# Strassen attention on one core: the order of the P·V products, the tiles that hold P, and the start

## The chip, the core and the metric

The kernel runs on one core of a Trainium2 chip. The core has a matrix engine (TensorE; PE for its matmuls, PEld for its weight loads), VectorE (DVE), ScalarE (ACT), GpSimd (POOL, which here issues the loads) and SyncE (SP, which here issues the stores and the DMA transpositions). Each engine runs its instructions in program order; between engines there are semaphores. The metric is the device time of one execution in microseconds (us).

## The reference

```
q, k, v: (8, 2048, 512) float32
scores = q @ k.transpose(0, 2, 1) / sqrt(512)
out    = softmax(scores, axis=-1) @ v          # (8, 2048, 512) float32
```

No maximum is taken off before the exp in the kernel; the sums of the exps come out of the second product, through a column of ones beside v.

## The kernel before

**Tiles.** A step g is one batch and 512 queries (32 steps, four to a batch). Its transposed probabilities P (2048 keys by 512 queries, fp16) are made block by block from QK products and lie in one tile `pt`, indexed by key block pair j, key half s and query. P times V gives four output blocks of 128 queries by 512, handled as two pairs, a and b.

**Winograd's form of Strassen.** Both matrix products replace eight half-size products by seven. So there are seven QK products for a group of four key blocks (class `Group`, 4 matmuls each, line 246, four groups a step) and seven PV products for a pair (class `Pair`, 8 matmuls each, line 328). DVE makes the sums and differences of blocks that serve as operands: of P in `p_sums` (s1, s2, a21 in place, s4, lines 289 to 293), of q, k and v in `q_sums`, `k_sums`, `v_sums` (the background sums). Several products of one pair add into the same PSUM bank, and between them the bank is read:

- bank x: products 1, 4, 6, 7; ACT scales it into the output after 3, 6 and 4, DVE adds it after 7
- bank z: products 5 and 3; ACT scales it after 5 (a DVE reciprocal of the row sums comes first), DVE takes another reciprocal after 3 and adds z after 6
- bank y: product 2; DVE adds it after 2

The scaling is line 336 (ACT), the add line 339 (DVE), the reciprocals lines 351 and 357. A pair's x comes from a ring of two banks; y and z have one bank each for both pairs.

**The main loop.** Step g's PV products run beside step g+1's QK products. A period has 28 slots. Each slot has one QK product in the order of `QORDER` (seven to a group, products 7 and 4 of a group one group later, as `prev`), and each odd slot has a PV product of `ORDER`, behind the QK product. After each QK product its reader is issued: copies by ACT (lines 259, 263, 266), adds by DVE (269, 272), exps by ACT (197; `exp_right` for two query halves at a time). The last group of a step ends in slots 0 to 5 of the next period.

**Loads.** `PLAN` gives slots to loads, transpositions (`dma_transpose`, line 112) and background sums, whose operations are issued one at a time in slots 0, 2, 3 and 6 of each seven. GpSimd and SyncE don't follow the slots: they run ahead as far as waits allow. q and k pass through a ring of staging tiles; v goes straight into `vh` (two buffers). `new_v` writes the column of ones into a new `vh` by a memset (line 168), and that memset waits until every reader of the buffer's old tile is done; the loads behind it on GpSimd's queue wait too. A step's q is loaded three steps ahead.

**The start.** q's first two blocks and k's first four are transposed by PE (line 125). Steps 0 and 1 are computed without Strassen (`plain_tile`, 4 matmuls of 512 columns and one exp a key block). Then step 0's remaining PV products run alone, and the main loop begins.

Of the kernel before, what the change touches and what calls it, by code (L numbers as in the profile page):

```python
# [12 lines left out]
def kernel(  # L13
# [21 lines left out]
    nc = tc.nc  # L35
    P = 128
    B, T, D = q.shape
# [22 lines left out]
    COPY = mybir.ActivationFunctionType.Copy  # L60

    const = ctx.enter_context(tc.tile_pool(name="const", bufs=1))
    stage = ctx.enter_context(tc.tile_pool(name="stage", bufs=3))
    kpool = ctx.enter_context(tc.tile_pool(name="kpool", bufs=5))
    qpool = ctx.enter_context(tc.tile_pool(name="qpool", bufs=3))
    vpool = ctx.enter_context(tc.tile_pool(name="vpool", bufs=2))
# [28 lines left out]
        "v": v.rearrange("b (n p) d -> b p n d", p=P),  # L95
    }

    def load(what, b, c):
        t = stage.tile([P, CH, D], F16, tag="stage")
        nc.gpsimd.dma_start(out=t[:], in_=srcs[what][b, :, c * CH:(c + 1) * CH, :])  # L100
        staged[what, b, c] = t

    def operands(what):
# [83 lines left out]
        ]  # L187

    def new_p(g):
        pt = ppool.tile([P, NJ, 2, QTW], F16, tag="pt")  # L190
        s1 = ppool.tile([P, NJ, QH], F16, tag="s1")
        s2 = ppool.tile([P, NJ, QH], F16, tag="s2")
        s4 = ppool.tile([P, NJ, QH], F16, tag="s4")
        pts[g] = (pt, s1, s2, s4)

    def exp(out_, in_):
        nc.scalar.activation(out=out_, in_=in_, func=EXP, scale=inv_sqrt_d)  # L197
# [1 line left out]
    def plain_tile(g, kb):  # L199

        b, qt = divmod(g, NQT)
        if kb == 0:
            new_p(g)
        st = bank("qz" if kb % 3 == 2 else "qx")
        c, n = divmod(kb, CH)
        for dc in range(ND):
            nc.tensor.matmul(
                st[:], kT[b, c][0][:, n, dc, :], qT[b, qt][0][:, :, dc, :],
                start=(dc == 0), stop=(dc == ND - 1),
            )  # L210
        exp(pts[g][0][:, kb // 2, kb % 2, :], st[:])

    class Group:

# [7 lines left out]
        def product(self, n):  # L222
            a11, a12, a21, a22 = k_blocks(self.a)
            b11, b12, b21, b22 = q_blocks(self.b)
            _, s1, s2, s4 = self.a
            _, t1, t2, t4 = self.b
            if n == 1:
                if self.n == 0:
                    new_p(self.g)
                self.pt = pts[self.g][0]  # L230
                self.x = bank("qx")
            elif n == 5:
                self.z = bank("qz")
            lhs, rhs, dst = {
                1: (a11, b11, "x"),
                2: (a12, b21, "y"),
                3: (s4, b22, "z"),
                4: (a22, t4, "x"),
                5: (s1, t1, "z"),
                6: (s2, t2, "x"),  # L240
                7: (a21, b12, "x"),
            }[n]
            dst = getattr(self, dst)
            for j in range(G):
                for c in range(2):
                    nc.tensor.matmul(  # L246
                        dst[:, j * QH:(j + 1) * QH], lhs[:, j, c, :], rhs[:, :, c, :],
                        start=(n in (1, 5) and j == 0 and c == 0), stop=(c == 1),
                        skip_group_check=True,
                    )  # L250
            getattr(self, f"after{n}", lambda: None)()
# [20 lines left out]
            nc.vector.tensor_add(self.cz[:, :, 0, :], self.two(self.z), self.cz[:, :, 0, :])  # L272

        def after4(self):
            exp(self.pt[:, self.js, 1, 0:QH], self.two(self.x))

        def after2(self):
            exp(self.pt[:, self.js, 0, 0:QH], self.two(self.y))

        def exp_right(self):  # L280
            exp(self.pt[:, self.js, :, QH:QTW], self.cz[:])

    def p_sums(g, n, part=None):
        pt, s1, s2, s4 = pts[g]
        js = slice(n * G, (n + 1) * G)
        a11, a21 = pt[:, js, 0, 0:QH], pt[:, js, 0, QH:QTW]
        a12, a22 = pt[:, js, 1, 0:QH], pt[:, js, 1, QH:QTW]
        if part in (None, 0):
            nc.vector.tensor_add(s1[:, js], a21, a22)  # L289
            nc.vector.tensor_sub(s2[:, js], s1[:, js], a11)  # L290
            nc.vector.tensor_sub(a21, a11, a21)  # L291
        if part in (None, 1):
            nc.vector.tensor_sub(s4[:, js], a12, s2[:, js])  # L293

    class Pair:

        def __init__(self, g, i):
            self.g, self.i = g, i  # L300

        def product(self, n):
            g, i = self.g, self.i
            pt, s1, s2, s4 = pts[g]
            vh, t1, t2, t4 = vs[g // NQT]
            c1 = slice(i * P, (i + 1) * P)
            c2 = slice(QH + i * P, QH + (i + 1) * P)
            if n == 1:
                self.x = bank("px")
            elif n == 2:  # L310
# [1 line left out]
            elif n == 5:  # L312
                self.z = bank("pz")
            lhs, rhs, dst = {
                1: (lambda j: pt[:, j, 0, c1], lambda j: vh[:, j, 0, 0:H], "x"),
                2: (lambda j: pt[:, j, 1, c1], lambda j: vh[:, j, 1, 0:H], "y"),
                3: (lambda j: s4[:, j, c1], lambda j: vh[:, j, 1, H:D + 1], "z"),
                4: (lambda j: pt[:, j, 1, c2], lambda j: t4[:, j, :], "x"),
                5: (lambda j: s1[:, j, c1], lambda j: t1[:, j, 0:H + 1], "z"),
                6: (lambda j: s2[:, j, c1], lambda j: t2[:, j, :], "x"),  # L320
                7: (lambda j: pt[:, j, 0, c2], lambda j: vh[:, j, 0, H:D], "x"),
            }[n]
            dst = getattr(self, dst)
            width = H + 1 if n in (3, 5) else H
# [18 lines left out]
        def store(self, o, half):  # L343
            b, qt = divmod(self.g, NQT)
            n = qt * NQS + half * (NQS // 2) + self.i
            nc.sync.dma_start(out=out[b, n * P:(n + 1) * P, :], in_=o[:])

        def after5(self):
            self.o2 = opool.tile([P, D], F32, tag="o")
            self.r2 = small.tile([P, 1], F32, tag="r2")  # L350
# [8 lines left out]

        def after2(self):  # L360
            self.final(self.o1[:, 0:H], self.y[:, 0:H], self.r1)

        def after6(self):
            self.scaled(self.o1[:, H:D], self.x[:, 0:H], self.r1)
            self.final(self.o1[:, H:D], self.z[:, 0:H], self.r1)
            self.store(self.o1, 0)

        def after7(self):
            self.final(self.o2[:, H:D], self.x[:, 0:H], self.r2)
# [2 lines left out]
            self.scaled(self.o2[:, 0:H], self.x[:, 0:H], self.r2)  # L372
            self.store(self.o2, 1)

    ORDER = "a1 b1 a5 a3 a2 a6 a7 b5 a4 b3 b2 b6 b7 b4".split()

    QORDER = ((0, 1), (1, 7), (0, 5), (0, 6), (1, 4), (0, 3), (0, 2))
    NS = len(QORDER) * NG
# [1 line left out]

    PLAN = {}
    for qt_, slot_, *what_ in (
        (0, 0, "newv"),
# [10 lines left out]
    for qt_ in range(NQT):  # L396
        PLAN.setdefault((qt_, 0), []).append(("load", "q", 3))
        PLAN.setdefault((qt_, 10), []).append(("trans", "q", 3))
        PLAN.setdefault((qt_, 15 if qt_ == 3 else 12), []).append(("sum", "q", 2))
    background = deque()  # L400

    def prefetch(g, slot):
        b, qt = divmod(g, NQT)
# [21 lines left out]


    NP = B * NQT
    load("q", 0, 0)
    load("k", 0, 0)
    load("k", 0, 1)  # L430
    dummy = bank("qy")
    pe_transpose("q", 0, 0)
    pe_transpose("k", 0, 0)
    load("k", 0, 2)
    load("k", 0, 3)
    new_v(0)
    nc.tensor.matmul(dummy[:], ident[:], kT[0, 0][0][:, 0], start=True, stop=True)
    load("q", 0, 1)
    for kb in range(NKB):
        plain_tile(0, kb)  # L440
# [1 line left out]
            pe_transpose("k", 0, kb // CH + 1)  # L442
        if kb % (2 * G) == 0 and kb:
            p_sums(0, kb // (2 * G) - 1)
        if kb == 3:
            load_v(0, 0)
        if kb == 7:
            load_v(0, 1)
        if kb == 11:
            load_v(0, 2)  # L450
            load_v(0, 3)
            load("q", 0, 2)
            load("q", 0, 3)
    pe_transpose("q", 0, 1)
    p_sums(0, NG - 1)

    pairs = (Pair(0, 0), Pair(0, 1))

    def pv(g, n):
        pairs[ORDER[n][0] == "b"].product(int(ORDER[n][1]))  # L460

    for kb in range(NKB):
        plain_tile(1, kb)
        if kb == 3:
            dma_transpose("q", 0, 2)
        if kb == 4:
            dma_transpose("q", 0, 3)
        if 6 <= kb < 14 and kb % 2 == 0:
            for f in v_sums(0, (kb - 6) // 2):
                f()  # L470
        if kb % (2 * G) == 0 and kb:
            p_sums(1, kb // (2 * G) - 1)
        if kb >= 14:
            pv(0, kb - 14)
    p_sums(1, NG - 1)
    for n in range(2, len(ORDER)):
        pv(0, n)
        if n < 6:
            for f in k_sums(0, n - 2):
                f()  # L480
        if n == 6:
            for f in q_sums(0, 2):
                f()
        if n == 7:
            for f in q_sums(0, 3):
                f()

    prev = None
    for g in range(1, NP):
        pairs = (Pair(g, 0), Pair(g, 1))  # L490
        for slot in range(NS):
            if g + 1 < NP:
                n, at = divmod(slot, len(QORDER))
                if at == 0:
                    cur = Group(g + 1, n)
                old, what = QORDER[at]
                if old == 0:
                    cur.product(what)
                elif prev is not None:
                    prev.product(what)  # L500
            elif slot in (1, 4):
                prev.product(QORDER[slot][1])
            if g + 1 < NP or slot < 7:
                at = slot % len(QORDER)
                if prev is not None:
                    if at == 2:
                        prev.exp_right()
                    if at == 4:
                        p_sums(prev.g, prev.n, 0)
                    if at == 5:  # L510
                        p_sums(prev.g, prev.n, 1)
                if at == len(QORDER) - 1 and g + 1 < NP:
                    prev = cur
            if slot % 2 == 1:
                pv(g, slot // 2)
            prefetch(g, slot)


# [28 lines left out]
```

## Time and profile before

| | us |
|---|---|
| median of 3 runs (lowest, highest) | 881.41 (880.58, 881.64) |
| the profiled execution | 881.62 |
| its span, first to last instruction | 879.5 |
| PE busy | 811.9 |
| DVE busy | 585.2 |
| ACT busy | 568.5 |

The rows are of that one execution. A row of the timeline gives start, duration, engine, source line, operation, tiles as out<-in, shapes, how many instructions were merged, and in brackets how long the engine stood idle before and which instruction's end released it. Matmuls overlap: the duration of a row ends later than the next row begins.

### The profile page before, as it was taken

The page shows a single profiled execution, that of the slowest core. Times are in us where ns is not written, and L with a number is a line of the kernel's source. Part 1 is how long each engine was busy: PE and PEld are TensorE (multiplying, and loading weights), DVE is VectorE, ACT ScalarE, POOL GpSimd, SP SyncE. Part 2 cuts the span into 40 slices and gives each one's busy share as a digit, 9 for nine tenths or more (in the row PEclk, how much of TensorE's full clock was granted, in tenths as well). Part 3 has the DMA queues.
Part 4 walks back from the last instruction along what each step waited for, and adds up shares of the span by engine and source line. Part 5 has one row for each costly group of instructions (what it writes and reads, how often), then busy time and mean ns, then how long its engine had stood idle before and what let it go on. Part 6 is the DMA issues. An engine that isn't in the chain of part 4 may idle for free.

```text
span 879.5 us, 18122 instructions
## 1 busy us (share of the span) xinstructions
PE 811.9 (92%) x7169; PEld 697.8 (79%) x7169; DVE 585.2 (67%) x1460; ACT 568.5 (65%) x1009; POOL 72.9 (8%) x116
## 2 busy tenths in 40 slices
PE   6979999999999999999999999999999999999997
PEld 4458878888887888888888888888888888888885
DVE  3675776776766777666776667767766767756653
ACT  2626666667666667666676676676676676666772
POOL 3200102001020000200001000200002000000000
PEclk9999999999999999999999999999999999999999
DMA  9994885948779593996939759296794958921101
GB/s 145 203 176 103 164 135 107 200 95 149 124 140 184 112 155 95 159 162 126 159 80 178 160 111 182 67 202 124 141 148 89 205 91 156 168 61 49 49 31 67
DMA packets 189989, 115.50 MB, mean 131 GB/s; under 512 B 124368, under 2 KB 173520, under 8 KB 189904
## 3 DMA queue, kind: packets, MB, share of 16 engines
q0 software_dynamic: 50688, 50.34, 37.9%
q1 hardware_dynamic: 139216, 64.01, 34.7%
q8 instruction: 56, 0.92, 0.4%
q14 instruction: 29, 0.24, 0.1%
HBM read 100.70 MB, written 33.55 MB: 153 GB/s over the span
## 4 chain that ended last, share of the span: by engine, by line
PE 61%; DVE 15%; ACT 14%; DMA 6%; issue 4%; POOL 0%; POOLq 0%; DVEq 0%; ACTq 0%
PE t L328 33%; PE t L246 28%; ACT pt L197 7%; ACT o L336 5%; DVE o L339 4%; DMA raw<-t 2%; DVE cz L272 2%; ACT cz L263 2%; DVE cz L269 2%; DMA t<-in_q_dram 2%; DVE s L289 2%; DMA t<-in_k_dram 2%; DVE pt L291 1%; DVE s L293 1%; DVE s L290 1%
## 5 line engine op out<-in xcount | busy, mean ns | idle before, releaser
L328 PEld LDWEIGHTS <-pt 128*128 128x128 f16 x2048 | 199.8, 98 | 71.8 <-issue 48.6
L336 ACT ACTIVATE o<-t,r 128x256 f32<-128x256 f32 x256 | 121.3, 474 | 171.1 <-DVE r L351 82.9
L328 PE MATMUL t<-vh,pt 128*128 128x256 f16 x1536 | 198.9, 273 | 14.0 <-ACT o L336 14.0
L197 ACT ACTIVATE pt<-t 128x512 f16<-128x512 f32 x272 | 163.6, 601 | 72.1 <-PE t L246 46.7
L246 PEld LDWEIGHTS <-raw 128*128 128x128 f16 x1920 | 187.7, 98 | 22.1
L246 PE MATMUL t<-raw 128*128 128x256 f16 x1440 | 196.7, 273 | 0.0
L328 PEld LDWEIGHTS <-s 128*128 128x128 f16 x1536 | 149.9, 98 | 42.7 <-issue 23.1
L246 PEld LDWEIGHTS <-ks 128*128 128x128 f16 x1440 | 140.8, 98 | 16.5
L339 DVE SCALAR_TENSOR_TENSOR o<-t,r,o 128x256 f32<-128x256 f32 x192 | 92.5, 482 | 91.9 <-ACT o L336 67.3
L246 PE MATMUL t<-qs,ks 128*128 128x256 f16 x960 | 134.3, 273 | 0.0
L328 PE MATMUL t<-t,s 128*128 128x257 f16 (+1 forms) x1024 | 133.1, 273 | 0.8 <-DVE o L339 0.8
L197 ACT ACTIVATE pt<-cz 128x1024 f16<-128x1024 f32 x120 | 127.4, 1061 | 2.3 <-DVE cz L269 1.1
L289 DVE TENSOR_TENSOR s<-pt 128x512 f16<-128x512 f16 x128 | 54.1, 423 | 95.7 <-ACT pt L197 95.7
L269 DVE TENSOR_TENSOR cz<-t,cz 128x512 f32<-128x512 f32 x120 | 82.5, 687 | 19.9 <-PE t L246 19.9
L263 ACT COPY cz<-t 128x512 f32<-128x512 f32 x120 | 70.1, 584 | 37.9 <-PE t L246 33.3
L328 PE MATMUL t<-t,pt 128*128 128x256 f16 x512 | 66.3, 272 | 22.8 <-DVE o L339 21.6
L272 DVE TENSOR_TENSOR cz<-t,cz 128x512 f32<-128x512 f32 x120 | 81.9, 683 | 4.7 <-PE t L246 4.7
L259 ACT COPY t<-t 128x512 f32<-128x512 f32 x120 | 68.4, 570 | 23.7 <-PE t L246 21.2
L328 PE MATMUL t<-vh,s 128*128 128x257 f16 x512 | 66.7, 273 | 17.5 <-ACT o L336 17.5
L246 PE MATMUL t<-qs,raw 128*128 128x256 f16 x480 | 72.1, 273 | 0.0
L246 PE MATMUL t<-raw,ks 128*128 128x256 f16 x480 | 72.1, 273 | 0.0
L266 ACT COPY cz<-t 128x512 f32<-128x512 f32 x120 | 69.5, 579 | 0.0
(34 smaller groups left out, 480.8 us busy)
## 6 DMA issues: line engine op xcount, KB each, us to landing
out_dram<-o SPq DMA_DIRECT2D x128, 256.0 KB, 2.8
t<-in_q_dram POOLq DMA_DIRECT2D x32, 512.0 KB, 7.9
t<-in_k_dram POOLq DMA_DIRECT2D x32, 512.0 KB, 7.4
vh<-in_v_dram POOLq DMA_DIRECT2D x32, 512.0 KB, 14.9
raw<-t SPq DMA_TRANSPOSE x58, 6.0
ident<-attn_identity SPq DMA_DIRECT2D x1, 32.0 KB, 1.8
```

What stands on the lines that cost most here:

```text
L197: nc.scalar.activation(out=out_, in_=in_, func=EXP, scale=inv_sqrt_d)
L246: nc.tensor.matmul(dst[:, j * QH:(j + 1) * QH], lhs[:, j, c, :], rhs[:, :, c, :], start=(n in (1, 5) and j == 0 and c == 0), stop=(c == 1) ...
L259: nc.scalar.copy(out=self.y[:], in_=self.x[:])
L263: nc.scalar.copy(out=self.cz[:, :, 1, :], in_=self.two(self.z))
L266: nc.scalar.copy(out=self.cz[:, :, 0, :], in_=self.two(self.x))
L269: nc.vector.tensor_add(self.cz[:, :, 1, :], self.two(self.x), self.cz[:, :, 1, :])
L272: nc.vector.tensor_add(self.cz[:, :, 0, :], self.two(self.z), self.cz[:, :, 0, :])
L289: nc.vector.tensor_add(s1[:, js], a21, a22)
L290: nc.vector.tensor_sub(s2[:, js], s1[:, js], a11)
L328: nc.tensor.matmul(dst[:, 0:width], lhs(j), rhs(j), start=(first and j == 0), stop=(j == NJ - 1), skip_group_check=True,)
L336: nc.scalar.activation(out=out_, in_=src, func=COPY, scale=r[:])
L339: nc.vector.scalar_tensor_tensor(out=out_, in0=src, scalar=r[:], in1=out_, op0=MULT, op1=ADD)
```

## The change

1. `ORDER`, the order of a step's 14 PV products, is new. A mark ' says that the product is one of the step before: b7 and b4 of a step run in slots 3 and 7 of the next period. The loop gets one more turn, for the last step's two. An output tile of the first half is stored when both of its halves are done (`store_first`), as 6 now comes before 2 in pair a.
2. `pt` becomes three tiles (`left[0]`, `left[1]`, `right`), so that each can be given back by itself. The plain tiles' exp becomes two.
3. The start: four staging tiles instead of three; the first q and k blocks are loaded in two pieces each; fourteen matmuls on a zeroed tile stand ahead of the first transposition in place of one on the identity; V's loads come one after every fourth plain tile of step 0; V's sums and the first PV products have other places in step 1; k's and q's sums after that go through the background queue, two at a time.

```diff
-    stage = ctx.enter_context(tc.tile_pool(name="stage", bufs=3))
+    stage = ctx.enter_context(tc.tile_pool(name="stage", bufs=4))
...
     def new_p(g):
-        pt = ppool.tile([P, NJ, 2, QTW], F16, tag="pt")
...
+        left = [ppool.tile([P, NJ, QH], F16, tag=f"left{s}", name=f"left{s}") for s in range(2)]
+        right = ppool.tile([P, NJ, 2, QH], F16, tag="right")
...
-        exp(pts[g][0][:, kb // 2, kb % 2, :], st[:])
+        left, right, _ = pts[g]
+        exp(left[kb % 2][:, kb // 2, :], st[:, 0:QH])
+        exp(right[:, kb // 2, kb % 2, :], st[:, QH:QTW])
...
         def after2(self):
             self.final(self.o1[:, 0:H], self.y[:, 0:H], self.r1)
+            self.store_first()
...
-    ORDER = "a1 b1 a5 a3 a2 a6 a7 b5 a4 b3 b2 b6 b7 b4".split()
+    ORDER = "a1 b7' a5 b4' a3 b1 a6 a2 a7 b5 a4 b3 b2 b6".split()
...
+    def pv(g, n):
+        which = ORDER[n]
+        g -= which.endswith("'")
+        if g < 0:
+            return
+        if which[1] == "1":
+            pairs[g, which[0]] = Pair(g, "ab".index(which[0]))
+        pairs[g, which[0]].product(int(which[1]))
...
+    load("q", 0, 0, 2)
+    load("k", 0, 0, 2)
     load("k", 0, 1)
+    load("k", 0, 2)
+
     dummy = bank("qy")
+    for n in range(14):
+        nc.tensor.matmul(dummy[:], warm[:, 0:P], warm[:], start=True, stop=True)
...
-        if 6 <= kb < 14 and kb % 2 == 0:
-            for f in v_sums(0, (kb - 6) // 2):
+        if kb in (6, 8, 10, 11):
+            for f in v_sums(0, (6, 8, 10, 11).index(kb)):
                 f()
...
-        if kb >= 14:
-            pv(0, kb - 14)
+        if kb in (11, 15):
+            pv(0, kb // 4 - 2)
+        if kb in (13, 14):
+            pv(0, kb - 11)
...
-    for n in range(2, len(ORDER)):
+    for n in range(4, len(ORDER)):
         pv(0, n)
...
+        if n < 8:
+            background.extend(k_sums(0, n - 4))
+        if n == 8:
+            background.extend(q_sums(0, 2))
+            background.extend(q_sums(0, 3))
+        if background:
+            background.popleft()()
+            background.popleft()()
...
-    for g in range(1, NP):
+    for g in range(1, NP + 1):
...
             if slot % 2 == 1:
-                pv(g, slot // 2)
+                if g < NP or ORDER[slot // 2].endswith("'"):
+                    pv(g, slot // 2)
```

## Rows read from the trace of the kernel before

**Rows 1.** The page: span; busy us and share by engine; granted clock in tenths.
```profile
span 879.5 us, 18122 instructions
...
PE 811.9 (92%) x7169; PEld 697.8 (79%) x7169; DVE 585.2 (67%) x1460; ACT 568.5 (65%) x1009; POOL 72.9 (8%) x116
...
PEclk9999999999999999999999999999999999999999
```
**Rows 2.** Waits of PE: who <- whom, total us, times, longest.
```profile
PE t L328 <- ACT o L336: 31.5, 66, 1.9
PE t L328 <- DVE o L339: 22.4, 25, 0.9
```
**Rows 3.** Timeline of PE, one period, its stops: b4, a3, b7, b4.
```profile
143.26 1.03 PE L328 MATMUL t<-t,pt 128*128 128x256 f16 x8 [0.93 <-DVE o L339]
...
150.88 1.04 PE L328 MATMUL t<-vh,s 128*128 128x257 f16 x8 [0.47 <-ACT o L336]
...
167.17 1.03 PE L328 MATMUL t<-vh,pt 128*128 128x256 f16 x8 [0.40 <-ACT o L336]
170.01 1.03 PE L328 MATMUL t<-t,pt 128*128 128x256 f16 x8 [0.93 <-DVE o L339]
```
**Rows 4.** Timeline of PE: first QK product of periods 1 and 31.
```profile
64.96 0.60 PE L246 MATMUL t<-raw 128*128 128x256 f16 x4
...
858.87 0.60 PE L246 MATMUL t<-raw 128*128 128x256 f16 x4
```
**Rows 5.** Timeline of PE, the end, no QK between: b3, b6, b7, b4.
```profile
869.66 1.04 PE L328 MATMUL t<-vh,s 128*128 128x257 f16 x8
...
871.54 1.03 PE L328 MATMUL t<-t,s 128*128 128x256 f16 x8
...
873.13 1.03 PE L328 MATMUL t<-vh,pt 128*128 128x256 f16 x8 [0.56 <-ACT o L336]
...
874.74 1.03 PE L328 MATMUL t<-t,pt 128*128 128x256 f16 x8 [0.58 <-DVE o L339]
```
**Rows 6.** Timeline of ACT and DVE, a period's beginning: exp_right, s1, scaling after a5.
```profile
146.99 1.06 ACT L197 ACTIVATE pt<-cz 128x1024 f16<-128x1024 f32 x1
...
148.08 0.43 DVE L289 TENSOR_TENSOR s<-pt 128x512 f16<-128x512 f16 x1 [2.19 <-ACT pt L197]
...
150.35 0.47 ACT L336 ACTIVATE o<-t,r 128x256 f32<-128x256 f32 x1 [1.33 <-DVE r L351]
```
**Rows 7.** Groups by line, the final add: busy us, mean ns, idle before.
```profile
L339 DVE SCALAR_TENSOR_TENSOR o<-t,r,o 128x256 f32<-128x256 f32 x192 | 92.5, 482 | 91.9 <-ACT o L336 67.3 <-PE t L328 19.4 <-ACT cz L263 4.5
```
**Rows 8.** Timeline of ACT: two scalings back to back.
```profile
58.48 0.84 ACT L336 ACTIVATE o<-t,r 128x256 f32<-128x256 f32 x2 [6.28 <-DVE r L351]
```
**Rows 9.** Timeline: memset of vh, q's transposition, first sum of that V.
```profile
141.56 0.13 POOL L168 MEMSET vh<- 128x8 f16 x1 [32.73 <-issue]
...
148.17 7.75 SPq L112 DMA_TRANSPOSE raw<-t  x1
...
163.35 0.41 DVE L183 TENSOR_TENSOR t<-vh 128x512 f16<-128x512 f16 x1
```
**Rows 10.** DMA issues at 142.8, 148.1 and 162.0 us: KB, us to landing.
```profile
vh<-in_v_dram POOLq DMA_DIRECT2D x1, 512.0 KB, 9.2
...
raw<-t SPq DMA_TRANSPOSE x1, 19.0
...
out_dram<-o SPq DMA_DIRECT2D x1, 256.0 KB, 8.1
```
**Rows 11.** Timeline, start: k's first transpositions, first tiles; a5 alone; q's sum.
```profile
9.70 1.89 PE L125 MATMUL tr<-ident,t 128*128 128x128 f16 x16 [0.66 <-DMA t<-in_k_dram]
...
11.90 2.56 PE L207 MATMUL t<-raw 128*128 128x512 f16 x8
...
46.63 1.04 PE L328 MATMUL t<-t,s 128*128 128x257 f16 x8
...
56.69 0.43 DVE L157 TENSOR_TENSOR qs<-raw 128x512 f16<-128x512 f16 x1 [0.65 <-DMA raw<-t]
```

More of the change, by code (lines that the diff above doesn't have):

```diff
@@ L96, with load @@
     }
-    def load(what, b, c):
+    def load(what, b, c, pieces=1):
         t = stage.tile([P, CH, D], F16, tag="stage")
-        nc.gpsimd.dma_start(out=t[:], in_=srcs[what][b, :, c * CH:(c + 1) * CH, :])
+        w = CH // pieces
+        for n in range(0, CH, w):
+            at = c * CH + n
+            nc.gpsimd.dma_start(out=t[:, n:n + w, :], in_=srcs[what][b, :, at:at + w, :])
         staged[what, b, c] = t
@@ L189, in new_p @@
     def new_p(g):
-        pt = ppool.tile([P, NJ, 2, QTW], F16, tag="pt")
[L191 to L194, printed above, removed]
+        left = [ppool.tile([P, NJ, QH], F16, tag=f"left{s}", name=f"left{s}") for s in range(2)]
+        right = ppool.tile([P, NJ, 2, QH], F16, tag="right")
+        sums = [ppool.tile([P, NJ, QH], F16, tag=f"s{n}", name=f"s{n}") for n in (1, 2, 4)]
+        pts[g] = (left, right, sums)
     def exp(out_, in_):
@@ L229, in product @@
                     new_p(self.g)
-                self.pt = pts[self.g][0]
+                self.left, self.right, _ = pts[self.g]
                 self.x = bank("qx")
@@ L274, in after4 @@
         def after4(self):
-            exp(self.pt[:, self.js, 1, 0:QH], self.two(self.x))
+            exp(self.left[1][:, self.js, :], self.two(self.x))
         def after2(self):
-            exp(self.pt[:, self.js, 0, 0:QH], self.two(self.y))
+            exp(self.left[0][:, self.js, :], self.two(self.y))
         def exp_right(self):
-            exp(self.pt[:, self.js, :, QH:QTW], self.cz[:])
+            exp(self.right[:, self.js], self.cz[:])
     def p_sums(g, n, part=None):
-        pt, s1, s2, s4 = pts[g]
+        left, right, (s1, s2, s4) = pts[g]
         js = slice(n * G, (n + 1) * G)
-        a11, a21 = pt[:, js, 0, 0:QH], pt[:, js, 0, QH:QTW]
-        a12, a22 = pt[:, js, 1, 0:QH], pt[:, js, 1, QH:QTW]
+        a11, a21 = left[0][:, js], right[:, js, 0]
+        a12, a22 = left[1][:, js], right[:, js, 1]
         if part in (None, 0):
-            nc.vector.tensor_add(s1[:, js], a21, a22)
-            nc.vector.tensor_sub(s2[:, js], s1[:, js], a11)
-            nc.vector.tensor_sub(a21, a11, a21)
+            add(s1[:, js], a21, a22)
+            sub(s2[:, js], s1[:, js], a11)
+            sub(a21, a11, a21)
         if part in (None, 1):
-            nc.vector.tensor_sub(s4[:, js], a12, s2[:, js])
+            sub(s4[:, js], a12, s2[:, js])
     class Pair:
         def __init__(self, g, i):
-            self.g, self.i = g, i
+            self.g, self.i, self.done = g, i, 0
         def product(self, n):
             g, i = self.g, self.i
-            pt, s1, s2, s4 = pts[g]
+            left, right, (s1, s2, s4) = pts[g]
             vh, t1, t2, t4 = vs[g // NQT]
-            c1 = slice(i * P, (i + 1) * P)
-            c2 = slice(QH + i * P, QH + (i + 1) * P)
+            cols = slice(i * P, (i + 1) * P)
             if n == 1:
@@ L314, in product @@
             lhs, rhs, dst = {
[L315 to L321, printed above, removed]
+                1: (lambda j: left[0][:, j, cols], lambda j: vh[:, j, 0, 0:H], "x"),
+                2: (lambda j: left[1][:, j, cols], lambda j: vh[:, j, 1, 0:H], "y"),
+                3: (lambda j: s4[:, j, cols], lambda j: vh[:, j, 1, H:D + 1], "z"),
+                4: (lambda j: right[:, j, 1, cols], lambda j: t4[:, j, :], "x"),
+                5: (lambda j: s1[:, j, cols], lambda j: t1[:, j, 0:H + 1], "z"),
+                6: (lambda j: s2[:, j, cols], lambda j: t2[:, j, :], "x"),
+                7: (lambda j: right[:, j, 0, cols], lambda j: vh[:, j, 0, H:D], "x"),
             }[n]
@@ L346, in store, with store_first @@
             nc.sync.dma_start(out=out[b, n * P:(n + 1) * P, :], in_=o[:])
+        def store_first(self):
+            self.done += 1
+            if self.done == 2:
+                self.store(self.o1, 0)
         def after5(self):
@@ L365, in after6 @@
             self.final(self.o1[:, H:D], self.z[:, 0:H], self.r1)
-            self.store(self.o1, 0)
+            self.store_first()
         def after7(self):
@@ L373, in after4 @@
             self.store(self.o2, 1)
-    ORDER = "a1 b1 a5 a3 a2 a6 a7 b5 a4 b3 b2 b6 b7 b4".split()
+    ORDER = "a1 b7' a5 b4' a3 b1 a6 a2 a7 b5 a4 b3 b2 b6".split()
     QORDER = ((0, 1), (1, 7), (0, 5), (0, 6), (1, 4), (0, 3), (0, 2))
     NS = len(QORDER) * NG
+    background = deque()
     PLAN = {}
@@ L399 @@
         PLAN.setdefault((qt_, 15 if qt_ == 3 else 12), []).append(("sum", "q", 2))
-    background = deque()
     def prefetch(g, slot):
@@ L427 @@
     NP = B * NQT
-    load("q", 0, 0)
-    load("k", 0, 0)
+    pairs = {}
+    def pv(g, n):
[6 more added lines that the diff above has]
+        pairs[g, which[0]].product(int(which[1]))
+    warm = const.tile([P, QTW], F16)
+    nc.vector.memset(warm[:], 0.0)
+    load("q", 0, 0, 2)
+    load("k", 0, 0, 2)
     load("k", 0, 1)
+    load("k", 0, 2)
     dummy = bank("qy")
+    for n in range(14):
+        nc.tensor.matmul(dummy[:], warm[:, 0:P], warm[:], start=True, stop=True)
     pe_transpose("q", 0, 0)
     pe_transpose("k", 0, 0)
-    load("k", 0, 2)
+    new_v(0)
     load("k", 0, 3)
-    new_v(0)
-    nc.tensor.matmul(dummy[:], ident[:], kT[0, 0][0][:, 0], start=True, stop=True)
     load("q", 0, 1)
@@ L444 @@
             p_sums(0, kb // (2 * G) - 1)
[L445 to L453, printed above, removed]
+        if kb % CH == 3:
+            load_v(0, kb // CH)
+    load("q", 0, 2)
+    load("q", 0, 3)
     pe_transpose("q", 0, 1)
     p_sums(0, NG - 1)
-    pairs = (Pair(0, 0), Pair(0, 1))
-    def pv(g, n):
-        pairs[ORDER[n][0] == "b"].product(int(ORDER[n][1]))
     for kb in range(NKB):
@@ L472 @@
             p_sums(1, kb // (2 * G) - 1)
-        if kb >= 14:
-            pv(0, kb - 14)
+        if kb in (11, 15):
+            pv(0, kb // 4 - 2)
+        if kb in (13, 14):
+            pv(0, kb - 11)
     p_sums(1, NG - 1)
-    for n in range(2, len(ORDER)):
+    for n in range(4, len(ORDER)):
         pv(0, n)
[L478 to L486, printed above, removed]
+        if n < 8:
[6 more added lines that the diff above has]
+            background.popleft()()
@@ L488 @@
     prev = None
-    for g in range(1, NP):
-        pairs = (Pair(g, 0), Pair(g, 1))
+    for g in range(1, NP + 1):
         for slot in range(NS):
+            n, at = divmod(slot, len(QORDER))
+            old, what = QORDER[at]
             if g + 1 < NP:
-                n, at = divmod(slot, len(QORDER))
                 if at == 0:
                     cur = Group(g + 1, n)
-                old, what = QORDER[at]
                 if old == 0:
                     cur.product(what)
[L499 to L513, printed above, removed]
+            if old == 1 and prev is not None:
+                prev.product(what)
+            if prev is not None:
+                if at == 2:
+                    prev.exp_right()
+                if at == 4:
+                    p_sums(prev.g, prev.n, 0)
+                if at == 5:
+                    p_sums(prev.g, prev.n, 1)
+            if at == len(QORDER) - 1:
+                prev = cur if g + 1 < NP else None
@@ L514 @@
             if slot % 2 == 1:
-                pv(g, slot // 2)
-            prefetch(g, slot)
+                if g < NP or ORDER[slot // 2].endswith("'"):
+                    pv(g, slot // 2)
+            if g < NP:
+                prefetch(g, slot)
 _INS = ['q', 'k', 'v']
```

## Prediction, made before the changed kernel ran

> **What bounds the kernel now.** Read the page first [rows 1]: TensorE (PE) is busy 92% of 879.5 us, VectorE (DVE) 67%, ScalarE (ACT) 65%, and the granted clock is full in every slice. So PE sets the end, and only what makes it idle can be won. Next PE's waits [rows 2]: 31.5 us until ACT line 336 (the scaling of an output half) and 22.4 us until DVE line 339 (the final add of one), 91 waits in all; besides them the view has only 8.8 us, at the start. Then PE's timeline of one period [rows 3]: the reader is to see three stops in 26.75 us (143.26 to 170.01): 0.47 before a3, 0.40 before b7, 0.93 before b4, each where a product of a pair adds into a bank that the product just before it in the same pair left to be read. Other products never stop, and no QK product (line 246) does.
>
> A row's length is 1.04 us for 8 matmuls where the next row starts 0.87 us later, so each stop costs its idle time and 0.17 more. From a3 at 150.88 to b7 at 167.17 lie 9 PV and 18 QK products, 144 matmuls: 16.29 - 0.57 = 15.72 us, 109.2 ns a matmul. I write u for a QK product (4 matmuls, 0.437 us); a PV product is 2u. A period is 224 matmuls, 24.46 us. Check: 26.75 less three stops (1.80 + 0.51) is 24.44.
>
> The main loop's 30 periods last from 64.96 to 858.87 [rows 4], 793.9 us; without stops 30 x 24.46 = 733.8. So 60.1 us is there to be won, 65.0 us lie before the loop and 20.6 after.
>
> **The braid.** QK products come in every slot, PV products in odd ones, so neighbours of the PV order have 2u = 0.87 us between them; with one PV product between, the gap is 6u = 2.62 us. What a bank's reader needs is seen where PE has nothing else to do, at the end [rows 5]: b3 to b6 with one product between 1.88 us start to start (own 0.87, so 1.01 after its end), b6 to b7 1.59 and b7 to b4 1.61 (0.72, 0.74). In the loop ACT and DVE are loaded, and the three stops show needs of 1.51, 1.44 and 1.97 us. In the new order a1 b7' a5 b4' a3 b1 a6 a2 a7 b5 a4 b3 b2 b6 every pair that shares a bank has another product between (a5-a3, a3-a6, a6-a7, a7-a4, b5-b3, b3-b6, b6-b7', b7'-b4'; so has b4' before b1, which takes its bank). 2.62 us is above all three needs: all stops go, -60.1 us.
>
> What is late next? I lay the durations of the rows along the new slots from a period's start S. The last group's tail is tightest. exp_right is issued in slot 2; in the period from 144.13 it ends at S+3.92, and s1 at S+4.38 [rows 6]. a5 reaches the matmuls that read it at S+10u+0.65 = S+5.02, so today 0.64 us are left. New is that b7' ends in slot 3 (S+3.49+0.17) and its final add (0.48 [rows 7]) lies ahead of s1 in DVE's queue with, in some periods, one background sum of 0.42: s1 then ends near S+4.97. Left: about 0.05 us. Behind it DVE does two sums, an add, s4 and the reciprocal by S+6.9, ACT scales a5's half by S+7.4 (today S+6.7), and a3 starts at S+18u = 7.86: 0.45 us left, where today it is stopped. The other edges keep 0.4 us (the copy after product 1 before product 6) to 1.4 us. Bounds for new stops: 0, and 0.9 us a period (DVE one add and one sum later), 27 us. I take 0.1, 3 us, since every edge comes out positive, if barely.
>
> **Weight blocks as tiles.** With b7' and b4' in the next period, pt as one tile would be held until slot 7 while its successor is written from slot 6. left ends with b2 in its own period; right is first written in slot 9, after b4'. So no wait. Loop instructions and their sizes stay: 0. In `plain_tile` (line 207 its matmuls) each exp of 512 columns becomes two of 256, in 32 tiles. No such exp is in the trace; the nearest row is the scaling of 128x256, 0.47 us [rows 6]: two, 0.95, against PE's 0.87 a tile would give ACT the lead, 32 x 0.08 = 2.6 us. But two of them back to back take 0.84 us together [rows 8], so the second adds 0.37, and 0.74 a tile stays below 0.87. I take 0 and keep 2.6.
> The Trainium skill (ScalarE: Activation LUTs, "What ACT_TABLE_LOAD costs") gives 186 + 0.833 N ns with constant operands, 93 ns more for each pointer operand, and 93 ns overlap; by it (an estimate) two exps add about 0.61 us a tile, and the term is 0 too.
>
> **The V buffer.** b7' reads vh and b4' reads t4 in the next period. The memset of a new vh waits for its old tile's last reader: today it runs at 141.56, as b7 ends, 2.57 us before S = 144.13 [rows 9]. New it runs after slot 3, S+3.6: 6.2 us later, six times, and GpSimd's queue behind it, the loads of q and V, with it. Today the transposition of that q starts at S+4.0 and lands 19.0 us on at S+23.0, the first V block, issued 1.3 us behind the memset, lands 9.2 us on [rows 10]. New: V block at S+14.1; DVE wants it in slot 20 (today 163.35, S+19.2 [rows 9]), now S+17.9: 3.8 us left, no wait. The transposition starts at S+10.2, lands at S+29.2, and the two stores behind it at about S+30.6 and S+32.1 (today the second of them lands 8.1 us after 162.05, S+26.0 [rows 10]). Its buffer is wanted by the scaling after the next period's a5, near S+31.4: ACT stands 0.7 us, of which PE sees about 0.5. 6 x 0.5 = 3 us; bounds 0 and 6 x 2.5 = 15.
>
> **Start.** Today the first key block's transpositions begin at 9.70 and the first tile at 11.90, its matmuls at half rate (8 in 2.56 us) [rows 11]. Fourteen matmuls on zeros and split loads let the tiles begin some 1.2 us earlier at full rate, until the next key block's landing binds; bounds 0 and 2.2; I take 1.2. The tiles keep their number; a1 and a5 stand among the second 16 as a1 and b1 do now, so the 12 products that today take 46.63 to 64.96 = 18.3 us become 10, from 45.4: 8.7 us of matmuls. There DVE leads: up to b3's reciprocal, on which b6 hangs, it has 4 sums of P and 14 background sums of 0.42 and 3 final adds of 0.48, 9.0 us from 46 on with reciprocals between; b6 starts near 56, the loop at 57. Also q's transposition landed only at 56.6, where DVE waited 0.65 us for it [rows 11], and the first QK product needs the same block; a little earlier loads allow 55.5. So 57.0 instead of 65.0, -8.0; bounds 54.6 (PE alone) and 61 (that landing 4 us later than today).
> The Trainium skill (DMA: Bandwidth & Descriptors, "Queues, rings and completion order") says that a DMA engine takes turns between its queue rows. The transposition's 19.0 us among loads [rows 10] agree. A fourth staging buffer lets one more load run beside the start's transpositions, which by this rule (an estimate) would start the loop up to 3 us later.
>
> **End.** Period 31 has the same 14 products, but b7' and b4' come last with b6, 1.59 + 1.61 us as today [rows 5], and the late reciprocal puts a3 0.4 us on: +0.5, so 21.1; bounds 0 and +1.5.
>
> **Sum.** 57.0 + 733.8 + 3 + 3 + 21.1 = 817.9 us of span. The profiled execution took 881.62 us for 879.5, so 2.1 lie around it: 820 us. The median of the runs shown, 881.41, is 0.2 below that execution, nothing here.
>
> **Rivals.**
> *The waits come back on DVE.* For: the 0.05 and 0.45 us left after exp_right are smaller than my errors; a stall there repeats in all periods. Against: DVE is idle a third of the time. At 0.5 to 0.9 us a period, 15 to 27 us instead of 3: 832 to 844.
> *The V loads come too late.* If the burst is 3.8 us slower than shifted, DVE's first V sum blocks its queue; each us beyond costs 6, and stores 2 us each: with 4 us, 24 + 12 more than forecast, 850. Against: the burst itself is unchanged.
> *The change doesn't do what it says:* the stops are ACT and DVE lagging in bulk, so they reappear at other products and only the start is won: 820 + 53, 873. For: stops name two engines. Against: ACT stood idle 1.33 us before the very scaling that a3 waits for [rows 6].
> *Slower:* the pauses keep PE at its full clock. If gapless work made the granted clock fall from 2.4 to 1.2 GHz in a share x of the 734 us, each us there yields half, so the loop grows by x times 734 us or more; from x = 8.5% it outweighs the 62 us, and 15% gives 930. For: the trace has no stretch without a pause much longer than the 16 us of [rows 3]. Against: the clock is full in all slices, at 92% busy [rows 1].
>
> **Chances.** Forecast 0.62 (its own range 812 to 831), DVE 0.20, V loads 0.08, only the start 0.05, clock 0.04, anything else near no change 0.01. The range 810 to 846 takes the first two whole and leaves 0.18 out. This kernel's measurement can tell 0.2%, 1.8 us. Faster 0.95, within 0.01, slower 0.04.
>
> **What would show it.** In the changed kernel's waits of PE, both lines gone from the loop; a period of 24.5 us between two starts; a memset of vh 3.6 us into every fourth period; the loop's first QK product at 55 to 59; stops of PE, if any, before a5 or a3 with DVE as releaser. A period above 25.3, or a loop that starts after 61, makes it wrong.

## The result and the profile after

The changed kernel takes 816.76 us (815.36 to 818.48 in four runs), the kernel before 881.52 in runs beside it: a ratio of 0.927 (95% interval 0.924 to 0.929). 820 us was predicted. The profiled execution took 816.5 us, of which 814.3 are span; read it part by part, by the same marks as before [rows 4]:

| us | before | after | change |
|---|---|---|---|
| before the loop (to the first QK product of period 1) | 64.96 | 57.54 | -7.42 |
| the loop's 30 periods | 793.91 | 735.46 | -58.45 |
| after it | 20.6 | 21.3 | +0.7 |
| span | 879.5 | 814.3 | -65.2 |

The page after has these lines for [rows 1]: the span, the busy time of PE, the granted clock in tenths, and the shares of the chain that ended last.

```profile
span 814.3 us, 18274 instructions
...
PE 800.5 (98%) x7182; PEld 698.9 (86%) x7182; DVE 586.7 (72%) x1461; ACT 559.6 (69%) x1041; POOL 74.3 (9%) x118
...
PEclk9999999999999999999999999999999999999999
...
PE 91%; DMA 4%; DVE 3%; ACT 1%; issue 0%; POOL 0%; ACTq 0%; DVEq 0%; POOLq 0%
```

PE's work is what it was, but for thirteen more matmuls on zeros; it now fills 98% of the span, 91% of the chain that ended last is its own, and the clock is full in every slice. PE's waits answer to [rows 2] (who <- whom, total us, times, longest; lines 331, 339 and 342 are the old 328, 336 and 339):

```profile
PE t L331 <- ACT o L339: 3.4, 6, 1.4
PE tr L128 <- DMA t<-in_k_dram: 2.2, 3, 1.3
PE t L331 <- DVE o L342: 1.4, 2, 0.8
```

The 91 stops and 53.9 us have become 8 stops and 4.8 us, and six of those, 4.1 us, lie outside the loop. The timeline of PE in a steady period answers to [rows 3]; these are b7', a5, b4', a3 and b1:

```profile
84.94 1.04 PE L331 MATMUL t<-vh,right 128*128 128x256 f16 x8
...
86.69 1.04 PE L331 MATMUL t<-t,s 128*128 128x257 f16 x8
...
88.44 1.04 PE L331 MATMUL t<-t,right 128*128 128x256 f16 x8
...
90.19 1.04 PE L331 MATMUL t<-vh,s 128*128 128x257 f16 x8
...
91.94 1.04 PE L331 MATMUL t<-vh,left 128*128 128x256 f16 x8
```

They stand 1.75 us apart, a PV and two QK products of 109.2 ns a matmul, with no bracket, that is no idle time. The loop's ends [rows 4], and, in the part after the loop, the two stops of [rows 5], where no QK product stands between; they are still there:

```profile
57.54 0.60 PE L250 MATMUL t<-raw 128*128 128x256 f16 x4
...
793.00 0.60 PE L250 MATMUL t<-raw 128*128 128x256 f16 x4
...
807.88 1.03 PE L331 MATMUL t<-vh,right 128*128 128x256 f16 x8 [0.56 <-ACT o L339]
809.48 1.03 PE L331 MATMUL t<-t,right 128*128 128x256 f16 x8 [0.57 <-DVE o L342]
```

### The profile page after: what moved, and what is told of

Read it like the earlier page. It is cut to its first block, busy times and chain, and to the rows that moved or that the text cites. A ratio compares the mean times of both kernels' runs of the same rounds, so it can differ in the third digit from the quotient of the medians.

```text
span 814.3 us, 18274 instructions
## 1 busy us (share of the span) xinstructions
PE 800.5 (98%) x7182; PEld 698.9 (86%) x7182; DVE 586.7 (72%) x1461; ACT 559.6 (69%) x1041; POOL 74.3 (9%) x118
## 4 chain that ended last, share of the span: by engine, by line
PE 91%; DMA 4%; DVE 3%; ACT 1%; issue 0%; POOL 0%; ACTq 0%; DVEq 0%; POOLq 0%
PE t L331 45%; PE t L250 44%; DMA out_dram<-o 3%; PE t L209 2%; DMA t<-in_k_dram 1%; ACT o L339 0%; PE tr L128 0%; POOL t L103 0%; ACT left L199 0%; DVE s L293 0%; DVE o L342 0%; DVE s L294 0%; DVE s L297 0%; ACT right L199 0%; ACT t L263 0%
## 5 line engine op out<-in xcount | busy, mean ns | idle before, releaser
L199 ACT ACTIVATE left<-t 128x512 f16<-128x512 f32 (+1 forms) x272 | 157.5, 582 | 37.2 <-PE t L209 21.9
L331 PE MATMUL t<-vh,left 128*128 128x256 f16 x1024 | 132.7, 273 | 0.0
L199 ACT ACTIVATE right<-cz 128x1024 f16<-128x1024 f32 x120 | 128.3, 1069 | 1.1 <-DVE cz L273 1.1
L331 PEld LDWEIGHTS <-right 128*128 128x128 f16 x1024 | 100.1, 98 | 14.4 <-issue 2.8
L331 PEld LDWEIGHTS <-left 128*128 128x128 f16 x1024 | 100.2, 98 | 11.8
L293 DVE TENSOR_TENSOR s<-right 128x512 f16<-128x512 f16 x128 | 53.9, 421 | 36.3 <-ACT right L199 31.8
```

Source lines behind the costliest of these rows:

```text
L331: nc.tensor.matmul(dst[:, 0:width], lhs(j), rhs(j), start=(first and j == 0), stop=(j == NJ - 1), skip_group_check=True,)
```

## The experiments

Edits are against the changed kernel. Four runs each, five for x8; the ratio is to the kernel before, run beside it (median 881.99 for x1 to x4, 881.16 for x5, x7, x8 and x9).

### x1: the old order, with the new tiles and start

```diff
-    ORDER = "a1 b7' a5 b4' a3 b1 a6 a2 a7 b5 a4 b3 b2 b6".split()
+    ORDER = "a1 b1 a5 a3 a2 a6 a7 b5 a4 b3 b2 b6 b7 b4".split()
```

> The changed kernel with the order of PV products of before (a1 b1 a5 a3 a2 a6 a7 b5 a4 b3 b2 b6 b7 b4, none moved to the next period); the three tiles of P and the new start stay. Theory (PE stops because a product adds into a bank that its neighbour left to be read, and the new order puts another product between): the three stops of a period come back, a period is 26.4 us in the mean instead of 24.5, 30 periods give back 55 to 60 us: 870 to 878 us. Rival (the separate tiles or the start carry the gain): 816 to 826 us.

877.32 us, ratio 0.994 (0.992 to 0.996). Its loop takes 793.86 us, against 793.91 before, and its waits of PE are nearly those of [rows 2]:

```profile
PE t L331 <- ACT o L339: 29.8, 66, 1.0
PE t L331 <- DVE o L342: 20.8, 23, 0.9
```

So all that the loop won is the order's; tiles and start alone only move the loop's first QK product to 60.62, 4.3 us earlier.

### x2: P in one tile again

```diff
-        left = [ppool.tile([P, NJ, QH], F16, tag=f"left{s}", name=f"left{s}") for s in range(2)]
-        right = ppool.tile([P, NJ, 2, QH], F16, tag="right")
+        pt = ppool.tile([P, NJ, 2, QTW], F16, tag="pt")
+        left = [pt[:, :, s, 0:QH] for s in range(2)]
+        right = pt[:, :, :, QH:QTW]
```

> The changed kernel with P in one tile again (left and right are slices of it); new order and new start stay. Theory as in the prediction: the tile is now given back only after b4' in slot 7, while the next step's first exp into it is issued in slot 6, so ACT waits until about 7.2 us into the period; in the changed kernel it gets to that exp at about 7.0 us anyway, behind the scaling after a5. So 0 to 0.3 us a period, 816 to 826 us. Rival (the separate tiles are what makes the move to the next period possible): a stop of 1 us or more in every period, 847 us or more.

819.32 us, ratio 0.928 (0.926 to 0.930). The loop takes 735.82 us, 0.36 more than with three tiles, which is no difference (the same loop takes 736.70 in x4's profiled run and 737.63 in x7's): the long hold of P costs nothing there, and my reason for the tiles is no condition of the gain. The other 2.1 us lie at the start, where k's first block came later. PE stood 2.77 us for it; the transpositions right behind are still fast, but from 12 to 14 us the granted clock is 0.50 of full speed, and the first tile takes 3.10 us instead of 1.89:

```profile
10.08 0.62 PE L128 MATMUL tr<-ident,t 128*128 128x128 f16 x8 [2.77 <-DMA t<-in_k_dram]
...
12.19 3.10 PE L210 MATMUL t<-raw 128*128 128x512 f16 x8
```

Whether this layout makes that load late isn't shown: the same wait, with the same first loads, is 1.48 us in x1's profiled run and 0.68 in x3's.

### x3 and x9: a3 behind a5 at once, and then with six output tiles

The prediction saw 0.45 us left between the scaling of a5's half and a3. These take that distance away: a3 moves from slot 9 to slot 7, b4' takes its place, and b1 and a6 change places. x9 has besides `opool` with 6 tiles in place of 4.

```diff
-    ORDER = "a1 b7' a5 b4' a3 b1 a6 a2 a7 b5 a4 b3 b2 b6".split()
+    ORDER = "a1 b7' a5 a3 b4' a6 b1 a2 a7 b5 a4 b3 b2 b6".split()
```

> The changed kernel with the order a1 b7' a5 a3 b4' a6 b1 a2 a7 b5 a4 b3 b2 b6: a3 stands right behind a5 again, all other neighbours share no bank. Theory (one neighbourhood is one stop): a stop before a3 alone. a3 would start 14u = 6.1 us into the period, and in the changed kernel ACT has scaled bank z at about 7.0 us: 0.9 us in each of 30 periods, 843 us (the old kernel's own stop there, 0.64 with the row's overhang, would give 836). Rival (the stops come from ACT and DVE lagging in bulk, and move about with any order): less than 0.2 us a period, under 823 us, or stops at other products too.

870.53 us, ratio 0.986 (0.983 to 0.989), some 27 more than I expected. The stop is where it should be. In 23 periods it is 0.59 or 0.93 us; in six it is 2.66 to 3.67 us, and in them ACT waits for a store. The second of these, first ACT's scaling after a5, then a3 and the products behind it on PE, then, by stretches, the busy time of PE, PEld, DVE, ACT and POOL, the granted clock, the DMA share and GB/s:

```profile
271.44 0.47 ACT L339 ACTIVATE o<-t,r 128x256 f32<-128x256 f32 x1 [3.52 <-DMA out_dram<-o]
```
```profile
268.27 1.04 PE L250 MATMUL t<-raw 128*128 128x256 f16 x8
271.96 1.30 PE L331 MATMUL t<-vh,s 128*128 128x257 f16 x8 [2.66 <-ACT o L339]
273.06 1.06 PE L250 MATMUL t<-raw 128*128 128x256 f16 x4
273.91 1.06 PE L250 MATMUL t<-qs,ks 128*128 128x256 f16 x4
```
```profile
270.00:272.00 2.00, 0.04 (x1) 0.04 (x1) 0.00 (x0) 0.56 (x2) 0.74 (x1) 1.00 1.14 285
272.00:275.00 3.00, 3.00 (x18) 2.23 (x18) 0.86 (x2) 1.44 (x3) 0.00 (x0) 0.60 1.19 248
```

Behind the stop the granted clock falls to 0.60 of full speed on average over 3 us, that is to the lower level of 1.2 GHz for most of them; four QK matmuls take 1.06 us instead of 0.60. The 32 matmuls from a3 at 271.96 to a6 at 277.13 take 5.17 us instead of 3.50: the slow stretch costs 1.7 us on top of a stop that is itself 1.7 longer than the ordinary 0.93. Behind four of the other five the matmuls are slow too; behind the first, 2.99 us at 168.29, they are not. Is it the store? x9 gives ACT two more output tiles:

> The kernel with a3 right behind a5 and six output tiles instead of four. With four it took 870 us: a stop of 0.8 to 1.1 us before a3 in every period, and in six periods one of about 4 us, where ACT waits for a store to land before it may write the next output tile, followed by a stretch at half the granted clock. Theory (the store wait, behind the late memset and loads of V, is what makes those six, and the clock falls because of them): with six tiles the six are like the others and the clock stays full, 842 to 848 us. Rival (the six come from late operands of V or q, whatever the output tiles): 865 us or more.

846.32 us, ratio 0.960 (0.958 to 0.962), as expected. ACT has no wait for a store any more, the mean granted clock of the profiled run is 0.999 instead of 0.987, and the same place of the same period shows only the plain stop:

```profile
PE t L331 <- ACT o L339: 27.1, 33, 1.3
```
```profile
265.33 1.04 PE L250 MATMUL t<-raw 128*128 128x256 f16 x8
267.29 1.04 PE L331 MATMUL t<-vh,s 128*128 128x257 f16 x8 [0.93 <-ACT o L339]
268.17 0.60 PE L250 MATMUL t<-raw 128*128 128x256 f16 x4
```

Its loop takes 762.1 us, 26.6 above the changed kernel's, or 0.89 a period; x3's takes 784.35. So one pair of neighbours without its distance costs 27 us, and the store wait with the slow clock behind it another 22: the six long stops are together 19.7 us, 14 above six of 0.93, and five slow stretches of 1.3 to 1.7 make the other 8.

### x4: the old start

```diff
-    stage = ctx.enter_context(tc.tile_pool(name="stage", bufs=4))
+    stage = ctx.enter_context(tc.tile_pool(name="stage", bufs=3))
...
-    load("q", 0, 0, 2)
-    load("k", 0, 0, 2)
+    load("q", 0, 0)
+    load("k", 0, 0)
...
-        if kb in (11, 15):
-            pv(0, kb // 4 - 2)
-        if kb in (13, 14):
-            pv(0, kb - 11)
+        if kb >= 14:
+            pv(0, kb - 14)
...
-    for n in range(4, len(ORDER)):
+    for n in range(2, len(ORDER)):
```

(and the rest of the start as before.)

> The changed kernel with the start of before: three staging tiles, loads in one piece, one matmul ahead of the transpositions, V's loads and sums and k's and q's sums where they stood. Order and tiles of the loop stay. Theory: the main loop begins 5 to 7 us later than the 57.5 us of the changed kernel (two products fewer in the stretch before it than before, so under the old 65.0), and nothing else changes: 822 to 824 us. Rival 1 (the start is hidden behind the loads of the second block of q, which the first QK products need): 817 us. Rival 2 (much of the gain is the start's): above 835 us.

826.01 us, ratio 0.936 (0.934 to 0.939), 2 us more than I expected: the start is worth 9.2 us by the medians and 8.0 by the profiled runs, 6.9 of them up to the loop's first QK product (64.44). Most of it is one long stop of PE that the new places of the sums avoid; the products behind it run at half rate, at a granted clock of 0.50 from 59.5 to 62:

```profile
PE t L331 <- DVE o L342: 4.9, 2, 4.3
```
```profile
59.49 1.87 PE L331 MATMUL t<-t,right 128*128 128x256 f16 x8 [4.33 <-DVE o L342]
61.15 1.60 PE L331 MATMUL t<-vh,s 128*128 128x257 f16 x8
62.58 1.04 PE L331 MATMUL t<-vh,left 128*128 128x256 f16 x8
```

Ahead of the add that ends this stop, DVE waits for q's transposition and then makes that block's sums and the next one's:

```profile
55.38 0.43 DVE L160 TENSOR_TENSOR qs<-raw 128x512 f16<-128x512 f16 x1 [1.34 <-DMA raw<-t]
```

An earlier stop of 2.04 us, before a3 at 47.78, has slow matmuls behind it too: the granted clock is 0.50 from 49 to 52 us.

### x5: two more sums on DVE ahead of s1

The tightest edge of the prediction was s1 before a5. Two adds of 0.44 us on a scratch tile in slot 3 of each period, 0.87 together, push s1 back.

```diff
+    scratch = const.tile([P, QTW], F16)
...
+            if slot == 3:
+                for _ in range(2):
+                    add(scratch[:], warm[:], warm[:])
```

> The changed kernel with two more DVE adds of 128x512 fp16 (on scratch, read by nothing) in slot 3 of each period, ahead of the last group's s1. Theory (the tightest edge is exp_right to s1 to a5, and in the changed kernel s1 ends 0.3 us before a5 reads it where background sums stand ahead, 0.6 to 1 us before where none do): s1 comes 0.8 us later, a5 stops 0.2 to 0.5 us a period, and the scaling before a3 keeps just ahead: 6 to 15 us, 823 to 832 us, with DVE as the releaser of a5. Rival (DVE stands idle 28% of the time and has room anywhere): 817 us.

832.67 us, ratio 0.945 (0.943 to 0.946), just above the upper edge of what I expected. PE's waits have one new line, once a period, and it names s1; the stop falls inside a5, before its last two matmuls (PE, then DVE):

```profile
PE t L331 <- DVE s L293: 12.3, 30, 0.6
```
```profile
285.90 0.82 PE L331 MATMUL t<-t,s 128*128 128x257 f16 x6
287.23 0.39 PE L331 MATMUL t<-t,s 128*128 128x257 f16 x2 [0.51 <-DVE s L293]
...
286.75 0.42 DVE L293 TENSOR_TENSOR s<-right 128x512 f16<-128x512 f16 x1
```

The loop grows by 15.2 us, 0.51 a period: of 0.87 us only some 0.36 were room, though DVE is idle more than a quarter of the time.

### x7: one matmul on zeros instead of fourteen

```diff
-    for n in range(14):
-        nc.tensor.matmul(dummy[:], warm[:, 0:P], warm[:], start=True, stop=True)
+    nc.tensor.matmul(dummy[:], warm[:, 0:P], warm[:], start=True, stop=True)
```

> The changed kernel with one matmul on zeros ahead of the first transposition instead of fourteen. Theory: the first transpositions and tiles run at half the granted clock, as in the old kernel (16 transpositions 1.89 us, 8 matmuls 2.56 us), so the second key block's transpositions begin at 14.3 us instead of 13.1 and everything behind is 1.2 us later: 818 us, the main loop from 58.7. Rival (the second key block lands at 13.0 anyway and binds): 817 us, the loop from 57.5 as in the changed kernel.

817.87 us, ratio 0.928 (0.927 to 0.930): not told apart from the change by time. The profile says more: the loop begins at 57.38, as by the rival. The first tile is slower, 2.48 us, yet the second key block's transpositions begin no later, at 12.88:

```profile
10.56 2.48 PE L209 MATMUL t<-raw 128*128 128x512 f16 x8
12.88 1.06 PE L128 MATMUL tr<-ident,t 128*128 128x128 f16 x16
```

The changed kernel has the faster tile and then waits for the load of that block:

```profile
10.99 1.89 PE L209 MATMUL t<-raw 128*128 128x512 f16 x8
13.06 1.07 PE L128 MATMUL tr<-ident,t 128*128 128x128 f16 x16 [0.18 <-DMA t<-in_k_dram]
```

So a faster first tile wins nothing here, as the next load binds. That the zeros make it faster isn't shown: x4 has no zeros either, and its first tile takes 1.89 us. Nor does the clock row show what slows the first matmuls in x7 and in the kernel before: it stands at 1.00 there, and only the durations tell.

### x8: a faster version

Six output tiles; q's second block transposed inside step 0's tiles; V's sums and half of k's issued earlier, among step 1's tiles; the other half of k's and q's last ones two at a time in period 1; and another order for the last step.

```diff
-    opool = ctx.enter_context(tc.tile_pool(name="opool", bufs=4))
+    opool = ctx.enter_context(tc.tile_pool(name="opool", bufs=6))
...
+    LAST = "a1 b7' a5 b4' a3 b1 a6 a2 b5 a7 b3 a4 b6 b2".split()
...
-        if kb in (6, 8, 10, 11):
-            for f in v_sums(0, (6, 8, 10, 11).index(kb)):
+        if kb in (1, 2, 3, 5):
+            for f in v_sums(0, (1, 2, 3, 5).index(kb)):
                 f()
...
+        if kb in (6, 9):
+            for f in k_sums(0, kb // 3 - 2):
+                f()
...
+        if n >= 12:
+            for f in q_sums(0, 2)[2 * (n - 12):2 * (n - 12) + 2]:
+                f()
+    background.extend(k_sums(0, 2) + k_sums(0, 3) + q_sums(0, 3))
```

> The changed kernel with a start and an end that follow the traces: V's sums earlier among the second plain tiles (1, 2, 3, 5) and the first two key blocks' sums among them too (6, 9), q's second-step sums last before the loop, the other key blocks' sums and q's next ones in the loop's first period (two at a time); q's second block transposed by PE inside the first plain tiles instead of behind them; six output tiles instead of four; and in the last step the order a1 b7' a5 b4' a3 b1 a6 a2 b5 a7 b3 a4 b6 b2. Theory: the stretch before the loop loses its stops of 1.4, 0.8 and 0.3 us, the copy behind the transposition 1.0, the first period's stops 1.2, the end one stop of 0.6: 811 to 813 us. Rival (the transposition of q's first loop block lands at 53.3 us and what follows it binds, and earlier work only waits for it): 815 to 817 us.

812.90 us (812.72 to 813.27), ratio 0.922 (0.921 to 0.924). The loop begins at 56.39, takes 733.52 us and 20.99 follow. (The loop's floor is 732.9 us: 30 x 24.46 is 733.8, but period 1 has no group of an earlier period to finish, so two QK products, 0.87 us, are missing in it.) The median is 3.9 us below the changed kernel's, and the ranges of the two don't overlap; which of the edits wins what was not tested singly. What PE still waits for on the PV path lies outside the loop:

```profile
PE t L331 <- ACT o L339: 3.3, 3, 1.5
...
PE t L331 <- DVE o L342: 0.8, 2, 0.6
```

## Why the prediction was right, step by step

**The braid: all stops go, -60.1 us.** Measured -58.45 in the loop, with what the next term leaves. x1 has the same loop as before without the order, x9 gives 27 us back by one pair of neighbours: the mechanism is the distance between two products of a pair on one bank.

**New stops, +3, and the V buffer, +3.** Here the sum was too high, and so was the floor under it, by the two QK products that period 1 doesn't have: 733.8 should have been 732.9. 735.46 is 2.5 us above that, for both terms. In the first period PE loses 1.2, all other 29 periods together about 1.3. The two stops that the loop's waits still name, 0.53 us at 65.50 and 0.17 at 261.88, are before a3, as foreseen, but ACT releases them, not DVE, and behind both ACT had waited for a store. The first:

```profile
64.98 0.47 ACT L339 ACTIVATE o<-t,r 128x256 f32<-128x256 f32 x1 [4.42 <-DMA out_dram<-o]
```

The edges behind exp_right came out as laid, a little wider. From a steady period (a5, s1, reciprocal, scaling, a3; its start S is 106.80):

```profile
111.17 1.04 PE L331 MATMUL t<-t,s 128*128 128x257 f16 x8
111.23 0.42 DVE L293 TENSOR_TENSOR s<-right 128x512 f16<-128x512 f16 x1
113.29 0.16 DVE L359 RECIPROCAL r<-t 128x1 f32<-128x1 f32 x1
113.49 0.47 ACT L339 ACTIVATE o<-t,r 128x256 f32<-128x256 f32 x1 [1.78 <-DVE r L359]
114.67 1.04 PE L331 MATMUL t<-vh,s 128*128 128x257 f16 x8
```

s1 ends at S+4.85 (laid out: 4.97), 0.17 us before the matmuls that read it at 111.17 + 0.65 (laid out: 0.05; x5 says 0.36 over all periods). The scaling ends at S+7.16 (7.4), 0.71 before a3 (0.45).

The V buffer did what the prediction said, with one consequence less. In the period from S = 229.20 and the next one, on POOL, then DVE, ACT and PE:

```profile
232.97 0.13 POOL L171 MEMSET vh<- 128x8 f16 x1 [37.13 <-issue]
```
```profile
260.18 0.16 DVE L359 RECIPROCAL r<-t 128x1 f32<-128x1 f32 x1
261.36 0.47 ACT L339 ACTIVATE o<-t,r 128x256 f32<-128x256 f32 x1 [2.78 <-DMA out_dram<-o]
261.88 1.04 PE L331 MATMUL t<-vh,s 128*128 128x257 f16 x8 [0.17 <-ACT o L339]
```

The memset runs at S+3.8 (3.6), q's transposition is issued at S+10.2 and lands at S+29.7 (29.2). The store behind it, issued at 247.91, lands 13.4 us later, at 261.3, and ACT starts its scaling 1.0 us after the reciprocal's end, where 0.7 was foreseen. But of that, 0.66 is the room just named (0.71, less the 0.05 between the end of a scaling and an a3 that waits for it), so PE is 0.34 us late and not 0.5, and in the other periods of this kind less or not at all. In ACT's waits that is much, in PE's next to nothing:

```profile
ACT o L339 <- DMA out_dram<-o: 18.0, 7, 4.4
```

The term's price stood on the room of another term, and I had put that one too low. x3 shows the other side: without the room, such store waits and the slow clock behind them cost 22 us.

**Tiles: 0.** Holds in the loop (x2). Each plain exp became two of 0.38 us of which the second starts 0.28 or 0.29 after the first, 0.66 a tile (laid out from two scalings back to back: 0.74), below PE's 0.87: no lead for ACT. The Trainium skill (ScalarE: Activation LUTs, "What ACT_TABLE_LOAD costs") gave 0.61 by estimate; the measured 0.66 decides, for the same answer. The reason given for the tiles, that one tile would be held too long, is not borne out.

**Start: -8.0.** Measured -7.4, at 57.54 instead of 57.0. Of my two parts, the earlier first tiles (1.2) are there by the number, but not by my reason: the second key block's transpositions begin at 13.06 instead of 14.29, yet at 12.88 without the zeros (x7) and at 13.25 without zeros and with the old loads (x4). What makes them earlier stays open; that the next block's landing binds came out as said. The later part, DVE leading up to b6, is right: the stops before the loop are 1.36, 0.83 and 0.34 us, all behind DVE's chain of sums, reciprocals and adds. That the loop might start up to 3 us later did not show: q's transposition, issued at 34.45, landed 18.9 us later, at 53.3.

**End: +0.5.** Measured +0.7; a3 of period 31 stops 0.44, laid out as 0.4.

Term by term the span was to be 817.9 us and is 814.3: the loop came out 4.3 under its terms, start and end 0.7 over theirs.

**The rivals.** DVE's waits did not come back, but x5 shows that 0.87 us more on DVE would have made 832.7, the lower end of that rival. V loads late: the burst was shifted, not slower (the first V block lands 8.5 us after its issue at 234.27, before 9.2), and DVE never waits for `vh`; the rival's sum should read 856 and not 850, on which nothing hangs. Only the start won: x1 is the reverse of it, 877. The clock: full in all slices at 98% busy, with 109.2 ns a matmul throughout, so gapless work does not lower it here. Where it fell (x2, x3, x4), a long stop stood ahead, though not each long stop did it.

## What to carry to other kernels

When an engine in the lead stops between two writes to one bank, put other work of it between them, and lay out the readers' chain slot by slot: what counts is the room on the few edges behind the latest result, not the idle share of the engine that makes them. Price a stall on a side engine only after taking off the room that its consumer still has; two stalls at one place add up only once that room is gone. And when PE does stop for a few microseconds, look at the granted clock behind the stop before you book the stop's length as its price.

## What the runs showed of the hardware

- A stop of PE can cost more than its length. In x3's loop the stops of 0.59 and 0.93 us left the granted clock at full; behind the one of 2.66 us it was at 1.2 GHz for most of the next 3 us, and 1.7 us were lost on top. The length of the stop alone doesn't decide: behind the one of 2.99 us the clock was full. x4's stops of 4.33 and 2.04 us and x2's of 2.77 us have a granted clock of 0.50 and slow matmuls behind them too, in x2 and behind the 2.04 us only after some fast ones. The Trainium skill (TensorE: Matmul & The Clock Gate, "What's actually happening") names 1.2 GHz as the clock that an idle PE falls back to; five of x3's six long stops agree in the level, and behind the sixth the clock did not fall.
- A store queued behind a DMA transposition of q lands late: the one issued at 247.91, 8.5 us behind a transposition's issue, takes 13.4 us, where the median of all stores of the changed kernel's profile is 3.8 us from issue to landing. In all six periods with V's burst such a store takes 12.7 to 13.4 us and lands 1 to 2.5 us after the transposition does. That it waits for the transposition fits this and isn't tested apart.
- 735 us of matmuls almost without a pause keep the full clock in the changed kernel: 0.9 or more in all 40 slices, 1.000 in the mean.
